# An mLSTM input projection as a first phase of seven products for eight, through DRAM

## The chip, the cores and the metric

The kernel runs on one core of one Trainium2 chip. The time of a run is the device time in microseconds (us). The metric is the median of a few runs: 2351.81 us before the change (three runs, 2350.69 to 2352.87 us). Engines are named as in the profile: PE is TensorE's matmul, PEld its weight load, DVE VectorE, ACT ScalarE, POOL GpSimd, and SP the engine whose queue issues nearly all DMAs.

## What is computed

The reference is a decoder trunk of two layers over 2048 tokens of width 1024, all in float32. Layer 0 has an mLSTM mixer, layer 1 a dilated attention over a shared K/V; after each mixer a gated embedding is added ("ple"). Cut to what the change touches:

```python
proj = rms_norm(h, norm_g) @ w_in            # 1024 -> 4104 columns
qk, v, o, z, gates = split(proj, [1024, 2048, 3072, 4096])
qk = silu(causal_depthwise_conv(qk, conv_w)) # 4 taps over tokens
q, k = split(qk, 2)                          # 4 heads of 128
ht = mlstm_chunkwise(q, k, v, i_pre, log_sigmoid(f_pre))
ht = rms_norm(sigmoid(o) * ht, hnorm_g)
h = h + (ht * silu(z)) @ w_out

def ple_add(h, p_l, ...):                    # after each mixer, p_l of width 256
    return h + (p_l @ w_proj) * sigmoid(rms_norm(h) @ w_gate)
```

## The kernel before, in words

Every large product is done in three matmuls for one: an operand is cut in a high part (`wh`, `xh`, float32r, written by ScalarE) and the rest (`wl`, `xl`, by VectorE), and TensorE adds `wh*xh`, `wl*xh` and `wh*xl` (helper `split`, lines 101 to 107; `project`, lines 150 to 173). A matmul has a 128x128 stationary operand and 512 moving columns. `project` runs over the pieces k of the inner dimension, loads and splits one 128x512 piece of the weights in each step, far ahead of its use (`high_priority(offset=PRE)`), and does 4 x 3 matmuls with it into four PSUM banks. There are eight banks. After each step it calls `pump()`, which takes one step of a generator in the list `side`: so work of another kind (mLSTM, attention) is written between two steps of a product. `drain()` takes all the steps that are left, with no product between them.

The program is written in this rough order, and the framework's scheduler sets each engine's own order from it, by priorities and by a model of its own:

- For each of four groups of 512 tokens: `a_in` (lines 323 to 432) projects the input to q, k (feature-major), the gates with a third of z, v, o and the rest of z (token-major, 344 columns a piece, `ZN`); the mLSTM of the group's four chunks of 128 tokens (`mlstm_pre`, `mlstm`) is pumped beside the products of v, o and z. `a_out` (lines 552 to 565) does the output product `w_out_a` (`mix_out`) and the embedding of layer 0 (`ple`: gate product `w_pg`, then the small product `w_p` of inner size 256). `b_in` (lines 581 to 644) projects to the shared K/V and to queries and z of layer 1, which go to DRAM.
- Beside the `b_in` of the last group and after it runs the attention; then, for each group, `mix_out` and `ple` of layer 1. In the very last `ple` the product `w_p` is written bank by bank (`by_tile`, lines 135 to 148).

In one chunk of the mLSTM, VectorE does a row part with scans (lines 470 to 483), the decay matrix (line 503, four instructions), two 512-wide products (497, 514) and, for each of four heads, the state (529), two small ones (532, 533) and the output (535); for each half the norm (546). TensorE does three 257-column matmuls for each head (525, 526, 528). A chunk's matmuls need the state of the chunk before.

Of the kernel before, what the change touches and what calls it, by code (L numbers as in the profile page):

```python
# [8 lines left out]
F32 = mybir.dt.float32  # L9
# [5 lines left out]
P = 128  # L15
# [9 lines left out]
ZN = 344  # L25
# [18 lines left out]
def trunk_kernel(ctx: ExitStack, tc: tile.TileContext, I: dict, O: dict, upto: int = 9):  # L44
# [23 lines left out]
    ready = {}  # L68
    with tc.high_priority(offset=2 * PRE):
# [22 lines left out]
    h2d = scratch("h2d", [NG, KD, P, T])  # L92
    kd = scratch("kd", [SEQ, 512])
# [40 lines left out]

    def by_tile(src, n, X, scale):

        W = []
        for k in range(len(X)):
            with tc.high_priority(offset=PRE):
                W.append(weights(src[k], n, scale))  # L140
        acc = []
        for i in range(NT):
            acc.append(bank())
            cs = slice(i * P, (i + 1) * P)
            for k, ((wh, wl), (xh, xl)) in enumerate(zip(W, X)):
# [45 lines left out]
    def sumsq(dst, src):  # L191
        jk = sm.tile([P, 512], BF16, name="jk", tag="jk", bufs=1)
        n = src.shape[-1]
        nc.scalar.activation(jk[:, :n], src, AF.Square, accum_out=dst)  # L194

    def pj(n=512):
        return sm.tile([P, n], F32, name="pj", tag="pj", bufs=8)

    def squares(acc, k, src, eng=nc.gpsimd):
# [3 lines left out]
        else:  # L203
            sq = sm.tile([P, T], F32, name="sq", tag="sq", bufs=2)
# [3 lines left out]
    def new_acc():  # L208
        return sm.tile([P, T], F32, name="acc", tag="acc", bufs=2)
# [10 lines left out]
    def spread(rst):  # L220
# [6 lines left out]
        for r in (rh.bitcast(F32), rl):  # L227
            dg = sm.tile([P, NT, P], F32R, name="dg", tag="sq", bufs=2)
# [5 lines left out]
    def row_rstd(parts, tag="rb"):  # L234
# [4 lines left out]
        rb = sm.tile([P, T], F32, name="rb", tag=tag, bufs=1)  # L239
# [31 lines left out]
    def ple(l, g, h, X, sq, done, hooks1={}):  # L271
        pT = []
        for k in range(2):
            with tc.high_priority(offset=PRE):
                praw = raw_piece(I["pT"][l, g, k], T)
                pT.append(new_x())
                split(*pT[k], praw, 1.0)
        st = {}
        hooks = rstd_hooks(st, sq, R1, R2)
        for grp in range(2):  # L280
# [9 lines left out]
            if (l, g, grp) == (1, NG - 1, 1):  # L290
                acc = by_tile(I["w_p"][l, grp], 512, pT, 0.5)
            else:
                acc = project(I["w_p"][l, grp], 512, 2, pT, True, 0.5)
            with tc.high_priority(offset=EVAC):
                for i in range(NT):
                    k = grp * NT + i
                    nc.vector.scalar_tensor_tensor(ths[i], ths[i], 1.0, acc[i], op0=ALU.add, op1=ALU.mult)
# [3 lines left out]
    pa = ExitStack()  # L301
    ap = pa.enter_context(tc.tile_pool(name="ap", bufs=1))
    tail = ap.tile([P, KD, 3], F32, name="tail")
    nc.vector.memset(tail, 0.0)
    cstate = ap.tile([P, NH, DV + 1], F32, name="cstate")
    nc.vector.memset(cstate, 0.0)
    mcar = ap.tile([NH, 1], F32, name="mcar")
    nc.vector.memset(mcar, 0.0)
    CQK = 0.25 * P ** -0.5

    ahead = {}

    def norms(g):

        sq = new_acc()
        for k in range(KD):
            raw = wp.tile([P, T], F32, name="xraw", tag="xraw", bufs=2)
            nc.sync.dma_start(raw, I["xT"][g, k])
            squares(sq, k, raw)
        ahead[g] = st = {}  # L320
        return rstd_hooks(st, sq, N1, N2, "rba")

    def a_in(g):
        X = []
        if g == 0:
            sq = new_acc()
        for k in range(KD):
            with tc.high_priority(offset=PRE):
                raw = raw_piece(I["xT"][g, k], T)
                X.append(new_x())  # L330
                split(*X[k], raw, gam[:, G_A, k:k + 1])
                if g == 0 and k < W0:
                    ready[k] = weights(I["w_q"][k], 512, 1.0)
                if g == 0:
                    squares(sq, k, raw, nc.vector)
        if g == 0:
            constants()
        if g:
            st, hooks = ahead.pop(g), {}
        else:  # L340
            st = {}
            hooks = rstd_hooks(st, sq, 5, 7)
        qk = ap.tile([P, 2 * NH, T], F32, name="qk", tag="qk", bufs=1)
        for s, seg in enumerate(("q", "k")):
            acc = project(I["w_" + seg], 512, 8, X, True, hooks=hooks if s == 0 else {})
            rst, rb = st["r"], st["rb"]
            us = []
            with tc.high_priority(offset=EVAC):
                for i in range(NH):
                    ct = s * NH + i  # L350
                    u = pj(T + 3)
                    us.append(u)
                    nc.gpsimd.tensor_copy(u[:, 0:3], tail[:, ct])
                    nc.vector.tensor_tensor(u[:, 3:], acc[i], rb, op=ALU.mult)
                    nc.gpsimd.tensor_copy(tail[:, ct], u[:, T:])
            for i in range(NH):
                ct = s * NH + i
                u = us[i]
                cv = pj()
                nc.scalar.mul(cv, u[:, 0:T], convw[:, ct, 0:1])  # L360
                for j in range(1, 4):
                    nc.vector.scalar_tensor_tensor(
                        cv, u[:, j:j + T], convw[:, ct, j:j + 1], cv, op0=ALU.mult, op1=ALU.add)
                nc.scalar.activation(u[:, 0:T], cv, AF.Tanh, scale=0.5)
                nc.vector.scalar_tensor_tensor(qk[:, ct], u[:, 0:T], 1.0, cv, op0=ALU.add, op1=ALU.mult)

        half = sm.tile([P, NT], F32, name="halfa", tag="halfa", bufs=2)
        nc.vector.tensor_scalar_mul(half, rst, 0.5)
        z = ap.tile([P, NT, DM], F32, name="z", tag="z", bufs=1)
        ga = sm.tile([P, NT, 8], F32, name="ga", tag="ga", bufs=2)  # L370

        def zproj(grp, hooks={}):
            acc = project(I["w_z"][grp], ZN, 8, X, False, hooks=hooks)
            w = ZN if grp < 2 else ZN - 8
            c0 = grp * ZN
            with tc.high_priority(offset=EVZ):
# [44 lines left out]
        for t in range(NT):  # L421
            times(t, 0, ZN)
# [503 lines left out]
```

## Time and profile before

| what | value |
| --- | --- |
| median of the runs | 2351.81 us |
| profiled execution: its own time, its span | 2347.66 us, 2345.8 us |
| granted TensorE clock, mean | 0.997 |
| busy: PE, DVE, ACT, POOL | 99%, 66%, 48%, 25% |
| DMA: bytes, mean rate | 337.14 MB, 144 GB/s |

The span runs from the first to the last instruction. "Busy" counts the union of an engine's instructions; consecutive matmuls overlap in the records, so the pace of TensorE is read from the starts of matmuls and not from their durations. In a group's row, "xcount" is the number of instructions, then come the busy time, the mean duration in ns, and the idle time of the engine ahead of them.

### The profile page before, as it was taken

How to read it: one execution, taken by the hardware profiler on the slowest of the kernel's cores; microseconds unless marked ns; L12 is line 12 of the kernel's file. 1: busy time of each engine (PE TensorE's matmuls, PEld its weight loads, DVE VectorE, ACT ScalarE, POOL GpSimd, SP SyncE). 2: the span in 40 equal slices, each digit the busy share in tenths (PEclk: the TensorE clock that was granted, in tenths of full speed). 3: DMA queues.
4: the chain of work that ended last, by engine and by line, in shares of the span. 5: the costliest groups of instructions: out<-in, count | busy, mean ns of one | idle time of the engine just before them, and what ended most of it. 6: DMA issues, size and time to landing. Idle time of an engine off the chain costs nothing.

```text
span 2345.8 us, 35374 instructions
## 1 busy us (share of the span) xinstructions
PE 2313.6 (99%) x11760; PEld 1977.5 (84%) x11760; DVE 1543.6 (66%) x3405; ACT 1128.3 (48%) x2731; POOL 593.0 (25%) x719
## 2 busy tenths in 40 slices
PE   9999999999999999999999999999999998999999
PEld 7889888888888888889888888888898887888887
DVE  6846665776566667747575675566755668786866
ACT  5434454543344545434444543344664666453643
POOL 5011235601211644011225601212202121220301
PEclk9999999999999999999999999999999999999999
DMA  5433344533244455333344543253674777465453
GB/s 184 125 91 115 99 149 162 183 116 121 61 123 125 146 164 165 117 91 111 103 130 142 174 125 120 64 171 117 203 221 134 231 237 228 135 198 164 145 160 98
DMA packets 190246, 337.14 MB, mean 144 GB/s; under 512 B 21552, under 2 KB 38256, under 8 KB 190064
## 3 DMA queue, kind: packets, MB, share of 16 engines
q1 hardware_dynamic: 189920, 334.86, 46.1%
q8 instruction: 93, 1.52, 0.3%
q14 instruction: 89, 0.73, 0.1%
q10 hardware_dynamic: 144, 0.02, 0.0%
HBM read 284.27 MB, written 50.53 MB: 143 GB/s over the span
## 4 chain that ended last, share of the span: by engine, by line
PE 85%; DVE 6%; DMA 4%; POOL 2%; ACT 2%; issue 1%; SPq 0%; ACTq 0%; DVEq 0%; POOLq 0%
PE bank L169 41%; PE bank L167 32%; PE bank L726 2%; PE bank L695 2%; PE bank L664 1%; DVE wl L104 1%; PE bank L525 1%; PE bank L526 1%; PE bank L528 1%; PE bank L715 1%; PE bank L182 1%; DMA oo<-o2d 1%; PE bank L512 1%; DMA o2d<-ot 1%; DVE xl L106 1%
## 5 line engine op out<-in xcount | busy, mean ns | idle before, releaser
L169 PE MATMUL bank<-wh,xh 128*128 128x512 f32 (+1 forms) x1664 | 642.5, 386 | 2.8 <-ACT wh L102 2.8
L169 PE MATMUL bank<-wl,xh 128*128 128x512 f32 (+1 forms) x1664 | 622.0, 374 | 0.8 <-DVE wl L104 0.8
L169 PE MATMUL bank<-wh,xl 128*128 128x512 f32 (+1 forms) x1664 | 622.6, 374 | 0.0
L102 ACT ACTIVATE wh<-wraw 128x512 fp32r<-128x512 f32 (+1 forms) x544 | 326.7, 603 | 549.5 <-PE bank L167 302.8
L104 DVE TENSOR_TENSOR wl<-wraw,wh 128x512 fp32r<-128x512 f32 (+1 forms) x512 | 353.9, 695 | 318.7 <-ACT wh L102 317.3
L167 PE MATMUL bank<-xh,wh 128*128 128x512 f32 x1272 | 501.9, 395 | 0.4 <-ACT xh L102 0.4
L167 PE MATMUL bank<-xh,wl 128*128 128x512 f32 x1272 | 496.0, 390 | 0.0
L167 PE MATMUL bank<-xl,wh 128*128 128x512 f32 x1272 | 495.9, 390 | 0.0
L169 PEld LDWEIGHTS bank<-wh,xh 128*128 128x128 f32 x1664 | 313.9, 189 | 51.0 <-ACT wh L102 3.1
L169 PEld LDWEIGHTS bank<-wh,xl 128*128 128x128 f32 x1664 | 313.4, 188 | 50.3
L169 PEld LDWEIGHTS bank<-wl,xh 128*128 128x128 f32 x1664 | 314.2, 189 | 49.3 <-DVE wl L104 1.2
L206 POOL TENSOR_TENSOR acc<-acc,sq 128x512 f32<-128x512 f32 x105 | 162.1, 1545 | 546.7 <-ACT sq L205 543.8
L167 PEld LDWEIGHTS bank<-xl,wh 128*128 128x128 f32 x1272 | 239.1, 188 | 50.5
L167 PEld LDWEIGHTS bank<-xh,wh 128*128 128x128 f32 x1272 | 239.4, 188 | 48.3 <-ACT xh L102 0.6
L167 PEld LDWEIGHTS bank<-xh,wl 128*128 128x128 f32 x1272 | 239.6, 188 | 47.8
L106 DVE SCALAR_TENSOR_TENSOR wl<-wraw,gam,wh 128x512 fp32r<-128x512 f32 x192 | 159.8, 833 | 154.1 <-ACT wh L102 151.5
L102 ACT ACTIVATE wh<-wraw,gam 128x512 fp32r<-128x512 f32 x192 | 138.0, 721 | 195.2 <-PE bank L169 134.8
L707 ACT ACTIVATE pr<-pr,nm 128x256 f32<-128x256 f32 (+1 forms) x192 | 86.6, 453 | 43.5 <-DVE nm L704 43.3
L601 POOL TENSOR_SCALAR ssb<-ssb,r 128x4 f32<-128x4 f32 x64 | 27.3, 426 | 254.1 <-ACT jk L194 233.0
L695 PE MATMUL bank<-kT,qT 128*128 128x128 f32 x600 | 78.5, 278 | 7.0 <-DVE pT L719 2.9
L695 PEld LDWEIGHTS bank<-kT,qT 128*128 128x128 f32 x600 | 72.8, 192 | 10.5 <-DVE pT L719 4.5
L726 PEld LDWEIGHTS bank<-vt,pT 128*128 128x128 f32 x600 | 75.3, 194 | 3.9
(413 smaller groups left out, 2957.4 us busy)
## 6 DMA issues: line engine op xcount, KB each, us to landing
wraw<-in_w_pg SPq DMA_DIRECT2D x128, 256.0 KB, 2.8
wraw<-in_w_in_b SPq DMA_DIRECT2D x128, 256.0 KB, 2.8
wraw<-in_w_z SPq DMA_DIRECT2D x96, 172.0 KB, 2.3
wraw<-in_w_v SPq DMA_DIRECT2D x64, 256.0 KB, 2.6
wraw<-in_w_o SPq DMA_DIRECT2D x64, 256.0 KB, 2.7
wraw<-in_w_out_a SPq DMA_DIRECT2D x64, 256.0 KB, 2.6
wraw<-in_w_kv SPq DMA_DIRECT2D x64, 256.0 KB, 2.7
kr<-kd SPq DMA_DIRECT2D x53, 256.0 KB, 4.2
```

The lines of the kernel that those rows point to most:

```text
L102: nc.scalar.mul(dst_h, src, scale)
L104: nc.vector.tensor_tensor(dst_l, src, dst_h.bitcast(F32), op=ALU.subtract)
L106: nc.vector.scalar_tensor_tensor(dst_l, src, scale, dst_h.bitcast(F32), op0=ALU.mult, op1=ALU.subtract)
L167: nc.tensor.matmul(acc[i], w[:, cs], x, start=first, stop=last)
L169: nc.tensor.matmul(acc[i][:, :n], x[:, cs], w, start=first, stop=last)
L182: nc.tensor.transpose(tp[:, t * P:(t + 1) * P], tiles[t][:, k * P:(k + 1) * P], ident)
L206: eng.tensor_tensor(acc, acc, sq, op=ALU.add)
L512: nc.tensor.matmul(sp[:, h * P:(h + 1) * P], qk[:, NH + h, ts_], qk[:, h, ts_], start=True, stop=True)
L601: nc.gpsimd.tensor_scalar(ss, ss, r2[:, t:t + 1], EPS, op0=ALU.mult, op1=ALU.add)
L695: nc.tensor.matmul(sp[:, hh * n + j * P:hh * n + (j + 1) * P], qT[:, hs], kvs[j]["k"][:, hs], start=True, stop=True)
L707: nc.scalar.activation(pr[:, hh, :n], pr[:, hh, :n], AF.Exp, bias=nm[:, h:h + 1], accum_out=md[:, 4 + h:5 + h])
L726: nc.tensor.matmul(op[:, hs], pTs[h // 2][:, c0 + j * P:c0 + (j + 1) * P], kvs[j]["v"][:, hs], start=j == 0, stop=j == nk - 1)
```

## The change

The projection (q, k, v, o, z of all tokens) moves ahead of everything else, into a phase of its own. It works on 1024 tokens at a time (`sb`) and on 1024 output columns at a time (`i`: q and k, z, o, v), inner size 1024. Each such product of 2x2 quarters (512 tokens, 512 inner, 512 columns) is made of seven quarter products instead of eight, numbered 1 to 7 and done in the order 1, 2, 5, 6, 7, 3, 4 (`PR`). The operands are sums and differences of quarters: those of x are made once for each `sb` and kept (`x_operand`), those of the weights for each product, on GpSimd (5, 7) and VectorE (6, 4) (`w_operand`), one product ahead. The results of 1, 5 and 6 are read from the running banks (`first`) and added later; finished tiles are scaled, passed through tanh where z and o need it, and written to DRAM (`ud`, `vad`, `oad`, `zad`). The gates have small products of their own (`gates`). The halves of a weight operand (128x1024 each, two for each product) have three buffers.

The small products `w_p` of both layers are moved too: those of layer 0 to the start of the first phase (`p_product`), those of layer 1 behind the first phase (`side_products`); their results go to DRAM (`pwd`), and `ple` loads them. Behind the first phase, the mLSTM of group 0 (`mixer(0)`) is pumped beside `side_products` and the rest of it is drained; `mixer(g + 1)` is pumped beside `a_out` and `b_in` of group g. A mixer loads its input from DRAM, four convolution taps included.

The core of the diff (line numbers that the text gives for new code are those of the changed file):

```diff
+    def x_operand(sb, p, accs):
+        ps = (5, 6) if p == 6 else (p,)
...
+        for kh in range(2):
+            ks = slice(2 * kh, 2 * kh + 2)
+            def put(q, t):
+                halves(new[q][0][:, ks], new[q][1][:, ks], t)
...
+            elif p == 6:
+                t, u = x_quarter(sb, 1, 0, kh, accs), x_quarter(sb, 1, 1, kh, accs)
+                nc.gpsimd.tensor_tensor(t, t, u, op=ALU.add)
+                put(5, t)
+                v = x_quarter(sb, 0, 0, kh)
+                sub(t, t, v, nc.vector)
+                put(6, t)
...
+    def w_operand(B, p):
+        out = []
+        for kh in range(2):
+            b = {(kq, nq): B[kq, nq, kh] for kq in range(2) for nq in range(2)}
...
+            elif p == 5:
+                t = b[0, 0]
+                sub(t, b[0, 1], t, nc.gpsimd)
+            elif p == 6:
+                t = B["t2", kh] = so.tile([P, 2, T], F32, name="t2", tag="t2", bufs=2)
+                sub(t, b[1, 1], b[0, 0], nc.vector)
...
+            out.append(w_half(t))
+        return out
+    def w_half(t):
+        hi, lo = (so.tile([P, 2, T], F32R, name=f"w{n}", tag=f"w{n}", bufs=3) for n in "hl")
+        halves(hi, lo, t)
+        return hi, lo
+    def multiply(X, W, acc, i, feat, first, last):
+        cs = slice(i * P, (i + 1) * P)
+        n = 2 * len(W)
+        for k in range(n):
+            wh, wl = (w[:, k % 2] for w in W[k // 2])
+            xh, xl = (x[:, k] for x in X)
+            for j, (w, x) in enumerate(((wh, xh), (wl, xh), (wh, xl))):
+                a, b = (w[:, cs], x) if feat else (x[:, cs], w)
+                nc.tensor.matmul(acc, a, b, start=first and k == 0 and j == 0,
+                                 stop=last and k == n - 1 and j == 2, skip_group_check=True)
...
+    p_weights(0)
+    for g in range(2):
+        p_operand(0, g)
+    x_operand(0, 1, accs[0])
...
+    p_product(0, 2)
+    p_product(0, 3)
+    fetch(0)
+    for p in (7, 3, 4):
+        x_operand(0, p, accs[0])
+    token_norm(0, accs[0])
+    for n, (sb, i, p) in enumerate(order):
+        with tc.high_priority(offset=60):
+            fetch(n + 1)
...
+        for j in range(NT):
+            multiply(XS[sb, p], W, dst[j], j, i == 0, start, stop)
+            with tc.high_priority(offset=EVAC):
+                if p in HALF:
+                    part[p, j] = first(HALF[p], j, dst[j])
+                else:
+                    h, nq, q = OUT[p]
+                    final(h, nq, j, dst[j], part.pop((q, j)) if q else None)
+        if i == 3 and sb == 0:
+            with tc.high_priority(offset=60):
+                x_operand(1, p, accs[1])
...
     def ple(l, g, h, X, sq, done, hooks1={}):
-            if (l, g, grp) == (1, NG - 1, 1):
-                acc = by_tile(I["w_p"][l, grp], 512, pT, 0.5)
-            else:
-                acc = project(I["w_p"][l, grp], 512, 2, pT, True, 0.5)
...
+                    pw = bg.tile([P, T], F32, name="pw", tag="pw", bufs=2)
+                    nc.sync.dma_start(pw, pwd[l, g, k])
+                    nc.vector.scalar_tensor_tensor(ths[i], ths[i], 1.0, pw, op0=ALU.add, op1=ALU.mult)
...
+    side.append(mixer(0))
+    for g in range(NG):
+        side_products(1, g)
+    drain()
+    Y, turn = turner(0)
+    turn(0, 1)
+    for g in range(NG):
+        hooks = {}
+        if g + 1 < NG:
+            side.append(mixer(g + 1))
+        X, sq = a_out(g, Y, turn)
+        if g + 1 < NG:
+            Y, turn = turner(g + 1)
+            b_in(g, X, sq, hooks=begin(Y, turn))
```

Where instructions stand now. First TensorE, in the mLSTM of group 0. Before, a head's three matmuls (lines 525, 526, 528) stood between steps of the product with the weights of o (line 169):

```order
L169 MATMUL bank<-wh,xl 128x512
L525 MATMUL bank<-v,ml 128x257 [waits Activation_49]
L526 MATMUL bank<-cstate,ml 128x257 [waits Pool_49]
L528 MATMUL bank<-v,ml 128x257 [waits Activation_49]
L169 MATMUL bank<-wh,xh 128x512
L169 MATMUL bank<-wl,xh 128x512 [waits DVE_49]
L169 MATMUL bank<-wh,xl 128x512
```

In the changed kernel this is the same place of group 0, in the drain behind the first phase (lines 697, 698 and 700 are a head's matmuls, 633, 634, 661, 667 and 684 those that prepare the next chunk):

```order
L697 MATMUL bank<-va,ml 128x257 [waits DVE_49]
L698 MATMUL bank<-cstate,ml 128x257
L700 MATMUL bank<-va,ml 128x257 [waits Activation_49]
L697 MATMUL bank<-va,ml 128x257 [waits DMAHW4_49,DVE_49,PE_49]
L698 MATMUL bank<-cstate,ml 128x257 [waits Pool_49]
L700 MATMUL bank<-va,ml 128x257
L633 MATMUL bank<-ident,gall 4x128 [waits Activation_49]
L634 MATMUL bank<-ident,gall 4x128
L697 MATMUL bank<-va,ml 128x257
L698 MATMUL bank<-cstate,ml 128x257
L700 MATMUL bank<-va,ml 128x257 [waits Activation_49]
L661 MATMUL bank<-ident,ra__5812 128x4 [waits DVE_49]
```

The products with 512 columns that stood between the heads are gone from this place: from the last 36 matmuls of `side_products` on, three of the four chunks follow each other alone. Second, SP's queue at the start. Before, the loads of x and of the first weights stood first in it:

```order
L111 DMA wraw<-in_xT 128x512
L111 DMA wraw<-in_w_q 128x512
L111 DMA wraw<-in_xT 128x512
L111 DMA wraw<-in_w_q 128x512
L111 DMA wraw<-in_xT 128x512
L78 DMA convw<-in_conv 128x32
L111 DMA wraw<-in_w_q 128x512 [waits DMAHW1_49,DVE_49,Activation_49]
```

In the changed kernel the first weights of the seven products (line 363) stand behind the loads of x (line 304) and the last stores of `p_product` (line 482):

```order
L304 DMA xr<-in_xT 128x2x512 [waits DMAHW5_49,DVE_49]
L482 DMA pwd<-st 128x512 [waits DMAHW6_49]
L482 DMA pwd<-st 128x512 [waits DMAHW7_49,Activation_49]
L482 DMA pwd<-st 128x512 [waits DMAHW0_49,DVE_49]
L482 DMA pwd<-st 128x512 [waits DMAHW1_49,Activation_49]
L482 DMA pwd<-st 128x512 [waits DMAHW2_49,DVE_49]
L482 DMA pwd<-st 128x512 [waits DMAHW3_49,Activation_49]
L482 DMA pwd<-st 128x512 [waits DMAHW4_49,DVE_49]
L482 DMA pwd<-st 128x512 [waits DMAHW5_49,Activation_49]
L363 DMA b_593<-in_s_in_a 128x1024 [waits DMAHW6_49]
L363 DMA b_595<-in_s_in_a 128x1024 [waits DMAHW7_49]
```

What the first of the seven products needs is now issued only when the load and the stores ahead of it have had their waits.

More of the change, by code (lines that the diff above doesn't have):

```diff
@@ new lines, in trunk_kernel, with sub, halves, stile @@
+    CQK = 0.25 * P ** -0.5
+    p1 = ExitStack()
+    xs = p1.enter_context(tc.tile_pool(name="xs", bufs=1, reuse_waits="tile"))
+    so = p1.enter_context(tc.tile_pool(name="so", bufs=1, reuse_waits="tile"))
+    banks = [bank() for _ in range(8)]
+    XS = {}
+    def sub(out, a, b, eng):
+        eng.tensor_tensor(out, a, b, op=ALU.subtract)
+    def halves(hi, lo, t):
+        nc.scalar.copy(hi, t)
+        nc.vector.tensor_tensor(lo, t, hi.bitcast(F32), op=ALU.subtract)
+    def stile():
+        return so.tile([P, T], F32, name="st", tag="st", bufs=10)
@@ new lines, in gate_weights, with gates @@
+    def gate_weights():
+        nc.sync.dma_start(wg, I["w_g"])
+        tmp = so.tile([P, 4, 8], F32, name="wgt", tag="wgt")
+        sub(tmp, wg[:, 4:8], wg[:, 0:4], nc.vector)
+        for q, t in enumerate((wg[:, 0:4], wg[:, 4:8], tmp)):
+            halves(wgs[:, q, :, 0:8], wgs[:, q, :, 8:16], t)
+    def gates(sb, h):
+        acc = banks[4 + h]
+        todo = ((XS[sb, 1], 0), (XS[sb, 2], 1)) if h == 0 else ((XS[sb, 5], 0), (XS[sb, 4], 2))
+        for q, (X, w) in enumerate(todo):
+            for k in range(4):
+                for j in range(2):
+                    nc.tensor.matmul(acc[0:16], wgs[:, w, k], X[j][:, k], start=q + k + j == 0,
+                                     stop=q == 1 and k == 3 and j == 1, skip_group_check=True)
+        t = stile()[0:16]
+        nc.scalar.copy(t, acc[0:16])
+        return t
@@ L434, in log_forget @@
+    p1.close()
     def log_forget(ga):
@@ L644, in b_in @@
                 nc.sync.dma_start(zd[rows(t), :], th)
-    for g in range(NG - 1):
-        b_in(g, *a_out(g, *a_in(g)))
-    X, sq = a_out(NG - 1, *a_in(NG - 1))
-    pa.close()
+    pb = ExitStack()
+    p2 = ExitStack()
+    ctx.enter_context(p2)
+    work(p2)
+    ap = pb.enter_context(tc.tile_pool(name="ap", bufs=1, reuse_waits="tile"))
+    cstate = ap.tile([P, NH, DV + 1], F32, name="cstate")
+    nc.vector.memset(cstate, 0.0)
+    mcar = ap.tile([NH, 1], F32, name="mcar")
+    nc.vector.memset(mcar, 0.0)
@@ new lines, in side_products @@
+    def side_products(l, g):
+        pT = []
+        for k in range(2):
+            with tc.high_priority(offset=PRE):
+                praw = raw_piece(I["pT"][l, g, k], T)
+                pT.append(new_x())
+                split(*pT[k], praw, 1.0)
+        for grp in range(2):
+            acc = project(I["w_p"][l, grp], 512, 2, pT, True, 0.5)
+            with tc.high_priority(offset=EVAC):
+                for i in range(NT):
+                    b = pj()
+                    (nc.scalar.copy if i % 2 else nc.vector.tensor_copy)(b, acc[i])
+                    nc.sync.dma_start(pwd[l, g, grp * NT + i], b)
```

443 lines of the change are left out of this document (277 added, 166 removed).

## The prediction

> **What bounds the kernel now.** I read the page first, then the windows by stage, then the chain of waits and the rows of single matmuls.
>
> ```profile
> span 2345.8 us, 35374 instructions
> PE 2313.6 (99%) x11760; PEld 1977.5 (84%) x11760; DVE 1543.6 (66%) x3405; ACT 1128.3 (48%) x2731; POOL 593.0 (25%) x719
> GB/s 184 125 91 115 99 149 162 183 116 121 61 123 125 146 164 165 117 91 111 103 130 142 174 125 120 64 171 117 203 221 134 231 237 228 135 198 164 145 160 98
> ```
>
> TensorE is busy for all but 32 us of the span, so a matmul less is time less, as long as nothing else comes to the front. The windows show where the 32 us are: the first `a_in`, and then a whole period of one group (from one turning of z to the next):
>
> ```profile
> core 0: us, PE busy (x) PEld busy (x) DVE busy (x) ACT busy (x) POOL busy (x), PEclk, DMA share, GB/s
> 0.00:226.50 226.50, 219.60 (x1089) 190.81 (x1090) 147.19 (x345) 99.42 (x216) 56.65 (x95) 0.98 0.41 123
> 226.50:666.80 440.30, 440.26 (x2097) 373.00 (x2097) 283.31 (x546) 203.37 (x473) 133.36 (x169) 1.00 0.42 130
> ```
>
> A period has no idle TensorE at all, with VectorE at 283/440. The pace of TensorE is in a row of the chain (start, us, line, count) and in two rows of the timeline that stand 54 matmuls apart, in the 344-column product:
>
> ```profile
> 681.74 43.57 PE bank L167 x192
> ```
>
> ```profile
> 65.72 0.32 PE L169 MATMUL bank<-wl,xh 128*128 128x344 f32 x1
> ...
> 74.00 0.32 PE L169 MATMUL bank<-wl,xh 128*128 128x344 f32 x1
> ```
>
> So a 512-column matmul costs 43.57/192 = 0.2269 us and a 344-column one 8.28/54 = 0.1533 us, whatever their durations say.
>
> **TensorE's saving.** Removed: q, k, v and o, 4 groups x 6 pieces x 8 steps x 12 = 2304 matmuls of 512, 522.8 us, and z with the gates, 1152 of 344, 176.6 us; together 699.4 us. Added: 2 x 4 x 7 products x 48 = 2688 matmuls and 64 for the gates, 2752 x 0.2269 = 624.4 us, and some 3 us of small transposes. That is **-72 us**. The 384 matmuls of `w_p` (87 us) only move, and so does the mLSTM.
>
> **Behind the first phase.** Here I see the largest price. From the last of the seven products to `w_out_a` of group 0, TensorE has 192 matmuls of `side_products` (43.6 us), four chunks of mLSTM and two turnings. The three matmuls of one head of a chunk stand here:
>
> ```profile
> 152.40 0.59 PE L525 MATMUL bank<-v,ml 128*128 128x257 f32 x2
> 152.83 0.60 PE L526 MATMUL bank<-cstate,ml 128*128 128x257 f32 x2
> 153.26 0.60 PE L528 MATMUL bank<-v,ml 128*128 128x257 f32 x2
> ```
>
> Starts are 0.43 us apart, so a head takes 1.3 us and a chunk 5.2, with some 1.7 of small ones 6.9 us; in all TensorE has 43.6 + 27.6 + 0.9 = 72 us. VectorE's work in the same stretch goes by these groups (count, busy and mean ns; I divide busy by count) and by the first and last of the eight row instructions of a chunk:
>
> ```profile
> L104 DVE TENSOR_TENSOR wl<-wraw,wh 128x512 fp32r<-128x512 f32 x416 | 304.7, 736 | 267.8 <-ACT wh L102 266.8
> L362 DVE SCALAR_TENSOR_TENSOR pj<-pj,convw 128x512 f32<-128x512 f32 x96 | 69.5, 761 | 0.1
> L365 DVE SCALAR_TENSOR_TENSOR qk<-pj 128x512 f32<-128x512 f32 x32 | 22.5, 715 | 3.8 <-ACT pj L364 3.5
> L666 DVE COPY qT<-bank 128x512 f32<-128x512 f32 x48 | 32.9, 686 | 5.8 <-PE bank L664 4.7
> L529 DVE SCALAR_TENSOR_TENSOR cstate<-cstate,dec,bank 128x257 f32<-128x257 f32 x64 | 30.1, 470 | 0.0
> L535 DVE SCALAR_TENSOR_TENSOR o<-bank,dn,o 128x256 f32<-128x256 f32 x64 | 30.8, 481 | 1.4
> L503 DVE SCALAR_TENSOR_TENSOR ml<-br,cols,masks 128x128 f32<-128x128 f32 x64 | 34.9, 602 | 27.0 <-DMA br<-rowd 27.0
> L546 DVE TENSOR_SCALAR o<-o,rr 128x256 f32<-128x256 f32 x64 | 20.0, 350 | 0.9
> L497 DVE SCALAR_TENSOR_TENSOR ml<-bank,cols 128x512 f32<-128x512 f32 x16 | 11.1, 692 | 6.5 <-PE bank L495 6.5
> ```
>
> ```profile
> 100.50 0.41 DVE L470 TENSOR_TENSOR_SCAN rb__1008<-ones,bank 4x128 f32<-4x128 f32 x1 [0.56 <-PE bank L462]
> ...
> 103.49 0.21 DVE L483 TENSOR_SCALAR rg__1011<-rg__1011 4x128 f32<-4x128 f32 x1
> ```
>
> One chunk: row part about 2.3, decay 2.2, two of 0.69, four heads at 0.47 + 0.48 + about 0.3 (5.0), norms 4 x 0.31 and small ones (2.0), and the product of z and o over 1024 columns, about 1.4 by line 104 doubled: 14.5 us, 58 for four. The convolution of group 0: 8 x (3 x 0.72 + 0.70) = 23 us; most of group 1's, which VectorE's order puts in here too: 22 taps and 6 ends, 20 us. `side_products`: 24 low parts at 0.72 (17 us), 16 results copied out of PSUM at 0.69 (11 us). Five low parts of `w_out_a` and a memset: 5 us. Sum 134 us, against TensorE's 72: this stretch is VectorE's. It begins only when the first phase's tiles are free and SP has issued the loads behind the last stores, 4 us by this row of the DMA issues (256 KB, 2.8 us) with ScalarE's first step behind it:
>
> ```profile
> wraw<-in_w_pg SPq DMA_DIRECT2D x128, 256.0 KB, 2.8
> ```
>
> With 10 us for waits of chunk on chunk the stretch takes 148 us: **+76 us** of idle TensorE. Bounds: 134 us without waits or entry (+62), 168 with waits doubled and 6 us more (+96).
>
> **Hand-overs in the first phase.** A product lasts 48 x 0.2269 = 10.9 us. Its second weight half takes the buffer that the product before it leaves six matmuls before its own end, and is needed six matmuls after the start: 12 x 0.2269 = 2.7 us for a ScalarE copy and a VectorE subtraction of 1024 columns. From 344 and 512 columns:
>
> ```profile
> L102 ACT ACTIVATE wh<-wraw 128x512 fp32r<-128x512 f32 x448 | 280.2, 628 | 474.4 <-PE bank L167 286.5 <-PE bank L169 116.2 <-issue 48.3
> L102 ACT ACTIVATE wh<-wraw 128x344 fp32r<-128x344 f32 x96 | 46.5, 486 | 75.1 <-PE bank L169 58.0 <-PE bank L167 16.4
> L206 POOL TENSOR_TENSOR acc<-acc,sq 128x512 f32<-128x512 f32 x105 | 162.1, 1545 | 546.7 <-ACT sq L205 543.8
> ```
>
> the copy is about 1.06 us, the subtraction 1.3 to 1.4 by line 104: it just fits. It no longer fits when GpSimd is at work, as VectorE's rows show, the first alone, the last beside GpSimd's:
>
> ```profile
> 269.30 0.69 DVE L104 TENSOR_TENSOR wl<-wraw,wh 128x512 fp32r<-128x512 f32 x1 [2.03 <-ACT wh L102]
> ...
> 272.42 1.73 DVE L104 TENSOR_TENSOR wl<-wraw,wh 128x512 fp32r<-128x512 f32 x1
> ```
>
> ```profile
> 272.01 4.99 POOL L206 TENSOR_TENSOR acc<-acc,sq 128x512 f32<-128x512 f32 x3 [15.42 <-ACT sq L205]
> ```
>
> The same instruction took 1.04 us longer. In the first phase GpSimd has 32 subtractions of 1024 columns (3.1 us each, line 206 doubled), some 56 scalings and additions of results and 14 squares (1.5 each) and 4 longer ones, about 220 of 610 us, 0.36. Of 56 hand-overs 20 meet it, at 0.9 us each: **+18 us**, bounds 0 and 62 (each waits out a whole subtraction). The Trainium skill, SBUF — State Buffer, section Who interferes with whom, has it as an exclusive lock: a VectorE instruction with two SBUF inputs and a GpSimd one that reads SBUF wait for each other's whole instruction; the trace agrees with blocking (1.73 for 0.69 us), and by that rule at its worst the term would be the 62 us.
>
> **The start.** `a_in` of group 0 takes 226.5 us; by count it has 576 x 0.2269 = 130.7, 288 x 0.1533 = 44.2, four chunks at 6.9 = 27.6 and some 3.5 of small ones, 206 in all, so 20.5 us go in its start-up. Now the first products need two loads of 512 KB for one of 256, and the sixth x operand has three tiles in three buffers: load 4, four squares at 1.5 us on GpSimd, its addition 3.1, two splits, some 15 us for each half behind ten earlier tiles (about 30 us). SP stands in that queue, so the first weights are issued at about 62, land at 66 and are split at 68 us; 43.6 of this are `w_p` products. 24.4 for 20.5: **+4 us**, bounds -8 and +20. Quarter 3 of the first tokens (x operands on VectorE and GpSimd), norm rows and gate columns: **+4**, 0 to 10.
>
> **`a_out` beside a mixer.** Three times the mLSTM of the next group now stands beside `a_out` and the first K/V product, 480 matmuls, with its own 27.6 us some 140 us of TensorE. What VectorE has there without it is read from the first window, what a loaded VectorE costs from the second:
>
> ```profile
> 262.00:345.00 83.00, 83.00 (x376) 69.00 (x375) 56.59 (x77) 40.29 (x69) 22.57 (x15) 1.00 0.44 134
> 1950.00:2100.00 150.00, 143.83 (x825) 124.00 (x824) 118.88 (x344) 78.99 (x197) 27.36 (x19) 1.00 0.59 184
> ```
>
> 56.59/83 over 110 us is 75 us, with 58 of mixer 133 of 140: 0.95. At 0.79 TensorE idles 4%. I take 4% here, 6 us a group: **+18 us**, bounds -3 and 45.
>
> **The end.** The last `w_p` product covered tanh and sums of the last gate product:
>
> ```profile
> 2333.53 2.73 DVE L287 TENSOR_TENSOR pj<-bank,rb 128x512 f32<-128x512 f32 x4 [4.76 <-PE bank L167]
> ...
> 2341.80 0.69 DVE L298 TENSOR_TENSOR h<-h,pj 128x512 f32<-128x512 f32 x1
> ```
>
> Before, behind the last matmul stood one bank's reading and addition (0.68 and 0.69) and the store, 3.3 us from the end of line 298 to that of the span: 4.7 us. Now the gate product's four banks end within 9 x 0.2269 = 2.0 us of each other, with twelve instructions of about 0.69 behind them: 8.3 - 2.0 + 3.3 = 9.6 us. As the first banks may be further along, I take **+4 us**, 0 to 8.
>
> At nothing: the DRAM traffic (by the tiles' sizes some 70 MB more, 30 GB/s over the span, where the slices above go from 61 to 237; uncovered it is part of the start's upper bound), and 90 more issues in SP's queue, beside 11 us of work for each product.
>
> **Sum.** -72 + 76 + 18 + 4 + 4 + 18 + 4 = +52 us. The profiled execution (span 2345.8, 1.9 us around it) would be 2399.7; it stands 4.1 under the median of the runs, so on the median 2351.8 + 52 = **2404 us**.
>
> **Rivals.** *The stretch behind the phase runs at TensorE's pace* (faster). For it: overlapping records, four of line 503 take 2.19 us for a mean of 0.602 each. Against it: 134 us are already busy time. With no idle there but the entry (+4) the time is 2332; it decides when the stretch takes under 95 us. Chance 0.20, of which 0.06 ends within 0.2% of 2351.8 (about what a measurement here can tell from no change).
>
> *TensorE's clock falls in the waits.* After a wait it was at half:
>
> ```profile
> 57.81 0.66 PE L169 MATMUL bank<-wh,xh 128*128 128x344 f32 x1 [2.83 <-ACT wh L102]
> ```
>
> ```profile
> 60.00:64.00 4.00, 4.00 (x15) 4.00 (x15) 3.30 (x6) 1.73 (x4) 0.18 (x1) 0.50 0.24 64
> ```
>
> Through the whole stretch, half speed doubles 72 us; with about 20 us of that on the chain from chunk to chunk, 2424. Chance 0.13. The Trainium skill, TensorE: Matmul & The Clock Gate, section HAM oscillation — how this bites in real kernels, says that idle gaps over about 3.4 us bring the half clock back; the trace shows it after 2.83 and 0.84 us.
>
> *Every hand-over that meets GpSimd waits out a whole subtraction:* 62 for 18 us, 2448. Chance 0.10; this is the rule of the lock above.
>
> **How the numbers follow.** The forecast has 0.57 (its own range 2375 to 2435). Slower: 0.57 + 0.13 + 0.10 = 0.80; same 0.06; faster 0.14. The range 2345 to 2455 leaves out most of the faster case and the top of the others.
>
> **What would show it.** Right: in the profile after, a stretch of about 148 us near 710 us with VectorE over 0.9 and TensorE near half; the seven products with waits for `wl` of some 1 us. Wrong: TensorE busy in that stretch; or a first phase much over 650 us; or `a_out` far longer than 146 us.

## The result and the profile after

The changed kernel takes 2537.51 us in the median of four runs (2532.66 to 2547.17), against 2352.34 us before: a ratio of 1.079 (95% interval 1.076 to 1.083), 185 us slower where the prediction had 52. The profiled execution is the longest of the four, 2547.17 us with a span of 2545.3. First the top of its page and its row of the granted clock:

```profile
span 2545.3 us, 33701 instructions
PE 2329.2 (92%) x11072; PEld 1923.4 (76%) x11072; DVE 1728.0 (68%) x3377; ACT 1166.1 (46%) x2644; POOL 745.9 (29%) x750
...
PEclk9799999999997789999899999999999999999999
```

TensorE has 688 matmuls less, and its busy time is not shorter but 16 us longer; in before it was 32 us short of the span, now it is 216. Where that is, the windows by stage show. The edges are the last of the seven products (756.1), the first `w_out_a` product (922.6), the first K/V product of groups 0 to 3 (1053.7, 1341.8, 1628.3, 1860.6) and the end, and inside the first phase the two places where x operands are made:

```profile
core 0: us, PE busy (x) PEld busy (x) DVE busy (x) ACT busy (x) POOL busy (x), PEclk, DMA share, GB/s
0.00:180.00 180.00, 147.02 (x584) 118.28 (x585) 142.01 (x141) 68.61 (x94) 83.99 (x50) 0.89 0.57 198
180.00:350.00 170.00, 170.00 (x750) 137.16 (x749) 90.38 (x123) 75.27 (x100) 52.59 (x26) 1.00 0.30 98
350.00:465.00 115.00, 98.70 (x407) 77.88 (x406) 100.76 (x98) 47.26 (x60) 42.80 (x23) 0.94 0.47 153
465.00:756.10 291.10, 291.10 (x1288) 237.18 (x1286) 137.93 (x172) 109.63 (x141) 76.43 (x41) 1.00 0.29 97
756.10:922.60 166.50, 99.06 (x367) 75.14 (x365) 116.21 (x267) 60.97 (x142) 29.00 (x66) 0.75 0.64 211
922.60:1053.70 131.10, 124.66 (x570) 100.83 (x571) 102.40 (x222) 53.75 (x124) 28.57 (x28) 0.96 0.42 137
1053.70:1341.80 288.10, 266.09 (x1177) 216.87 (x1175) 210.82 (x405) 136.03 (x350) 106.19 (x140) 0.95 0.48 156
1341.80:1628.30 286.50, 265.28 (x1175) 216.12 (x1174) 210.72 (x406) 136.45 (x351) 106.16 (x139) 0.96 0.47 154
1628.30:1860.60 232.30, 228.74 (x1024) 189.05 (x1023) 147.92 (x233) 112.11 (x279) 94.75 (x122) 0.99 0.49 157
1860.60:2545.30 684.70, 638.51 (x3745) 554.89 (x3743) 468.87 (x1318) 366.01 (x1008) 125.44 (x117) 0.98 0.59 188
```

In the steady parts of the seven products TensorE keeps its pace: 1288 matmuls in 291.1 us, 0.226 each. At the start 584 x 0.2269 = 132.5 of 180 us are matmuls, at the change of tokens 407 x 0.2269 = 92 of 115, and VectorE is busy for 0.79 and 0.88 of these. Behind the phase and beside `a_out` the clock is down too.

Three stages of the kernel before with the same edges, for the comparison (from turning z to the first K/V product; one period from K/V to K/V, which here includes an input projection; from the last K/V product to the end):

```profile
226.50:327.00 100.50, 100.46 (x459) 83.01 (x459) 65.43 (x97) 45.45 (x77) 16.50 (x12) 1.00 0.40 126
327.00:767.40 440.40, 440.35 (x2098) 373.06 (x2097) 283.40 (x547) 203.38 (x473) 133.45 (x168) 1.00 0.42 130
1646.70:2345.80 699.10, 673.94 (x3937) 585.83 (x3935) 480.77 (x1338) 377.23 (x1029) 125.05 (x117) 0.99 0.58 180
```

From these and the prediction's terms (an input projection of a group 174.8 us, `w_p` 10.9, a mixer's matmuls 27.6, all by count) the forecast of each stage can be laid beside what came:

| stage | forecast | measured | difference |
| --- | --- | --- | --- |
| first phase: 671 of matmuls + 20.5 + 26 | 717.5 | 756.1 | +39 |
| stretch behind it | 148 | 166.5 | +19 |
| `a_out` of group 0: 100.5 - 10.9 + 27.6 + 6 | 123.2 | 131.1 | +8 |
| period 0 to 1: 440.4 - 174.8 - 10.9 + 6 | 260.7 | 288.1 | +27 |
| period 1 to 2 | 260.7 | 286.5 | +26 |
| period 2 to 3, no mixer: 440.4 - 174.8 - 10.9 - 27.6 | 227.1 | 232.3 | +5 |
| rest: 699.1 - 43.6 + 4 | 659.5 | 684.7 | +25 |

The rows differ by 149 us; the profiled execution, 2547.17, lies 147.5 us above the 2399.7 forecast for it.

### The profile page after: what moved, and what is told of

Same layout as the page of the kernel before. It is cut to its first block, busy times and chain, and to the rows that moved or that the text cites. A ratio compares the mean times of both kernels' runs of the same rounds, so it can differ in the third digit from the quotient of the medians.

```text
span 2545.3 us, 33701 instructions
## 1 busy us (share of the span) xinstructions
PE 2329.2 (92%) x11072; PEld 1923.4 (76%) x11072; DVE 1728.0 (68%) x3377; ACT 1166.1 (46%) x2644; POOL 745.9 (29%) x750
## 4 chain that ended last, share of the span: by engine, by line
PE 60%; DVE 18%; DMA 8%; POOL 5%; issue 5%; ACT 3%; SPq 1%; POOLq 0%; ACTq 0%; DVEq 0%
PE bank L406 19%; PE bank L159 16%; PE bank L157 15%; PE bank L993 2%; DVE wl L109 2%; PE bank L962 2%; DMA pj<-ud 2%; DMA xr<-in_xT 1%; DVE xr L314 1%; PE bank L931 1%; DVE h L280 1%; DVE wl L111 1%; DVE xl L111 1%; DVE pj L863 1%; DMA oo<-o2d 1%
## 5 line engine op out<-in xcount | busy, mean ns | idle before, releaser
L157 PE MATMUL bank<-xl,wh 128*128 128x512 f32 x960 | 382.5, 402 | 5.0 <-DVE xl L111 3.3
L157 PE MATMUL bank<-xh,wl 128*128 128x512 f32 x960 | 384.1, 400 | 0.0
L159 PE MATMUL bank<-wh,xh 128*128 128x512 f32 x768 | 308.1, 401 | 0.0
L159 PE MATMUL bank<-wh,xl 128*128 128x512 f32 x768 | 301.9, 393 | 0.0
L159 PE MATMUL bank<-wl,xh 128*128 128x512 f32 x768 | 301.4, 392 | 0.0
L406 PE MATMUL bank<-wl,xh 128*128 128x512 f32 x672 | 264.5, 394 | 8.9 <-DVE wl L295 8.9
L406 PE MATMUL bank<-wh,xh 128*128 128x512 f32 x672 | 263.8, 393 | 7.0 <-ACT wh L294 7.0
L406 PE MATMUL bank<-wh,xl 128*128 128x512 f32 x672 | 263.7, 392 | 0.0
L107 ACT ACTIVATE wh<-wraw 128x512 fp32r<-128x512 f32 x240 | 149.8, 627 | 228.2 <-PE bank L157 171.3
L109 DVE TENSOR_TENSOR wl<-wraw,wh 128x512 fp32r<-128x512 f32 x224 | 168.4, 754 | 124.2 <-ACT wh L107 123.2
L295 DVE TENSOR_TENSOR wl<-b,wh 128x1024 fp32r<-128x1024 f32 x96 | 126.7, 1321 | 95.8 <-ACT wh L294 94.3
L159 PEld LDWEIGHTS bank<-wh,xl 128*128 128x128 f32 x768 | 145.4, 189 | 30.7
L159 PEld LDWEIGHTS bank<-wh,xh 128*128 128x128 f32 x768 | 145.8, 190 | 28.7
L406 PEld LDWEIGHTS bank<-wl,xh 128*128 128x128 f32 x672 | 127.4, 190 | 38.9 <-DVE wl L295 12.2
```

The costliest lines, as they stand in the source:

```text
L107: nc.scalar.mul(dst_h, src, scale)
L109: nc.vector.tensor_tensor(dst_l, src, dst_h.bitcast(F32), op=ALU.subtract)
L157: nc.tensor.matmul(acc[i], w[:, cs], x, start=first, stop=last)
L159: nc.tensor.matmul(acc[i][:, :n], x[:, cs], w, start=first, stop=last)
L295: nc.vector.tensor_tensor(lo, t, hi.bitcast(F32), op=ALU.subtract)
L406: nc.tensor.matmul(acc, a, b, start=first and k == 0 and j == 0, stop=last and k == n - 1 and j == 2, skip_group_check=True)
```

## The experiments

The theories: **A**, VectorE's work, spread over the whole kernel before, now stands bunched at a few places, and TensorE waits there; **B**, the chains (chunk on chunk, the way of row numbers through DRAM and back) have no cover wherever they stand; **C**, the half clock behind the waits is the larger part; **D**, the DRAM traffic behind the phase. All verdicts are medians, against the 2537.5 us of the changed kernel; stage lengths come from the profiled executions. As the changed kernel's profiled execution stands 9.7 us above its median, the gains of its stages can add up to some 10 us more than those of the medians. The stretch from the last of the seven products to the first K/V product, which several runs are compared with, is in the changed kernel:

```profile
756.10:1053.70 297.60, 223.72 (x936) 175.96 (x935) 218.61 (x488) 114.72 (x265) 57.57 (x94) 0.85 0.54 178
```

**half_pump.** The mixers at every second step of a product:

```diff
+    def halved(steps):
+        for _ in steps:
+            yield
+            yield
...
-            side.append(mixer(g + 1))
+            side.append(halved(mixer(g + 1)))
         X, sq = a_out(g, Y, turn)
```

> The mixers of groups 1 to 3 take a step only at every second step of the products, so they are spread over a_out and b_in. Theory A (VectorE's work is bunched: in the changed kernel VectorE is at 151 of 180 us beside a_out with a mixer, and at about 0.55 in the b_in behind it): of the some 37 us that TensorE loses in each of the three groups 20 to 30 go, so 2537.5 - 75 = 2460 us, 2445 to 2485. Theory B (the chain from chunk to chunk and its loads from DRAM set the pace, wherever they stand): the same waits come back between other steps, 2525 to 2545. Theory C (the half clock behind each wait is the larger part): the same as A in sign, but at most 8 us a group, 2510 to 2520.

Measured: 2493.89 us (ratio 1.061, 1.059 to 1.063), 43.6 less. The first of the two periods with a mixer in its windows, and the last period, in which no mixer begins:

```profile
1024.80:1292.90 268.10, 256.40 (x1175) 209.30 (x1174) 209.94 (x406) 132.86 (x350) 102.16 (x140) 1.00 0.52 168
...
1560.60:1809.90 249.30, 246.13 (x1123) 203.09 (x1122) 176.89 (x330) 121.41 (x319) 97.84 (x133) 1.00 0.49 160
```

The same matmuls (1175 records for 1177) with the same VectorE time (209.94 for 210.82) take 268.1 for 288.1 us: where the mixer's work stands decides, not how much of it there is. That is A in sign, but the run moves the chain too, which now has twice as many steps of a product between its own. The size is between A's and C's; the last period is 17 us longer (249.3 for 232.3), as a part of the last mixer moved into it: 1123 matmuls for 1024.

**late_mix.** The mixers only beside `b_in`:

```diff
-        if g + 1 < NG:
-            side.append(mixer(g + 1))
         X, sq = a_out(g, Y, turn)
         if g + 1 < NG:
+            side.append(mixer(g + 1))
```

> The mixers of groups 1 to 3 start only when a_out of the group before is done, so all of a mixer stands beside b_in. Theory A (VectorE's work is bunched): a_out alone loses nothing, but b_in, with VectorE at 0.55 without the mixer, now has some 100 us of mixer and convolution in about 160 us, so part of the loss only moves: 2505 us, 2480 to 2530. Theory B (chain of chunks): no gain, 2525 to 2550.

Measured: 2584.15 us (1.101, 1.098 to 1.104), 46.6 us slower than the changed kernel, which neither theory had. The longest wait of the first period stands at the beginning of the mixer. TensorE, then what VectorE waited for there:

```profile
1079.66 1.23 PE L697 MATMUL bank<-va,ml 128*128 128x257 f32 x2 [14.28 <-DVE ml L686]
```

```profile
1076.06 2.15 DVE L675 SCALAR_TENSOR_TENSOR ml<-br,cols,masks 128x128 f32<-128x128 f32 x4 [10.48 <-DMA br<-rowd]
```

TensorE stands in order behind a chunk whose row numbers are still on their way through DRAM, with VectorE idle for 10.48 us: that is B's wait. In the changed kernel the longest wait of the same period is on the same line, and it is another:

```profile
1265.13 1.23 PE L697 MATMUL bank<-va,ml 128*128 128x257 f32 x2 [8.78 <-DVE ml L686]
```

```profile
1257.91 4.16 DVE L675 SCALAR_TENSOR_TENSOR ml<-br,cols,masks 128x128 f32<-128x128 f32 x4
```

There VectorE has no pause during the whole wait: instructions for other products stand ahead of the chunk's, and the four of line 675, beside sums on GpSimd, take 4.16 us for 2.15. So beside the products both can count: A in the changed kernel, B in late_mix. What GpSimd's part is worth in this stage was not tested.

**wp1_back.** `w_p` of layer 1 in `ple` again, as in before:

```diff
-    for g in range(NG):
-        side_products(1, g)
     drain()
...
+            if l and (g, grp) == (NG - 1, 1):
+                acc = by_tile(I["w_p"][l, grp], 512, pT, 0.5)
+            elif l:
+                acc = project(I["w_p"][l, grp], 512, 2, pT, True, 0.5)
```

> The small products w_p of layer 1 stand in the last stage again, as before the change, and not behind the first phase. Theory A (VectorE sets the pace of the stretch behind the phase, and w_p covered waits of the attention at the end): the stretch is shorter by VectorE's 28 us to TensorE's 44 us; the last stage gets 43.6 us of matmuls of which some 25 fill waits: together -10 to -25, 2520 us. Theory B (the stretch is as long as the chain of chunks and its loads, the products only fill its waits): the stretch stays, the last stage is longer by 18 us, 2555 us.

Measured: 2515.29 us (1.070, 1.068 to 1.073), 22.2 less. From the last of the seven products to the first K/V product, and from the last K/V product to the end:

```profile
756.00:1001.60 245.60, 169.23 (x744) 133.62 (x743) 195.08 (x448) 92.50 (x225) 59.02 (x92) 0.83 0.47 156
...
1810.40:2518.70 708.30, 678.78 (x3937) 589.96 (x3935) 484.28 (x1342) 379.01 (x1032) 126.07 (x117) 0.99 0.56 178
```

The first is 52 us shorter (245.6 for 297.6), more than either theory gave, and the second has all of its 192 matmuls back (43.6 us) and is only 23.6 longer (708.3 for 684.7). So 20 us of `w_p` had filled waits of the attention; moving it out gave only the other half. The median is in A's range, but 52 is more than VectorE's 28 and more than TensorE's 43.6: something else was relieved. The DMA view of the first 84 us behind the phase, in the changed kernel, suggests what (issues: count, KB each, us to landing):

```profile
DMA packets 12309, 23.39 MB, mean 278 GB/s; under 512 B 1293, under 2 KB 2321, under 8 KB 12304
...
pwd<-pj SPq DMA_DIRECT2D x25, 256.0 KB, 3.7
wraw<-in_w_p SPq DMA_DIRECT2D x16, 256.0 KB, 4.8
```

This gave theory D.

**no_store.** The stores of `side_products` left out:

```diff
                     (nc.scalar.copy if i % 2 else nc.vector.tensor_copy)(b, acc[i])
-                    nc.sync.dma_start(pwd[l, g, grp * NT + i], b)
...
-                    nc.sync.dma_start(pw, pwd[l, g, k])
+                    nc.sync.dma_start(pw, pwd[0, g, k])
```

> The results of side_products are not stored (32 stores of 256 KB left out; ple of layer 1 loads those of layer 0 in their place), all else as in the changed kernel. Theory D (in the first 84 us behind the first phase 23.4 MB pass at 278 GB/s, and the loads and stores set the pace there): 8.4 MB less are 30 us less: 2508 us. Theory A (VectorE sets the pace there): its work is the same: 2530 to 2540.

Measured: 2521.67 us (1.072, 1.070 to 1.074), 15.8 less; the stretch to the first K/V product is 280.6 for 297.6 us. Half of D's 30, with VectorE's work unchanged: the stores that I had put at nothing cost some 16 us here. Whether by their traffic is not shown: they also stand in SP's queue ahead of the mixer's loads, and they keep tiles of the same eight buffers (`pj`) that these loads need. In the changed kernel's first 84 us the largest of SP's waits for a result that it is to store is this row (us in total, times, longest), and the third load of the mixer's input is issued at 788.0 us, in no_store at 776.1:

```profile
SPq L842 <- DVE pj L841: 9.9, 4, 6.8
```

**scale_act.** The scaling of x on ScalarE:

```diff
-            nc.vector.tensor_scalar(t[:, j], t[:, j], gam[:, G_A, k0 + j:k0 + j + 1], None, op0=ALU.mult)
+            nc.scalar.mul(t[:, j], t[:, j], gam[:, G_A, k0 + j:k0 + j + 1])
```

> The scaling of x by the norm's weight in the first phase (72 instructions of 128x512, mean 1.09 us beside GpSimd where the shortest take 0.40) is done by ScalarE instead of VectorE. Theory A (VectorE is what TensorE waits for at the start, 40 to 180 us, and at the change of tokens, 350 to 460 us; it loses 71 us of work there): 25 to 45 us go, 2500 us. Theory B (loads of x and GpSimd's sums set the pace there): 2530 to 2540.

Measured: 2522.73 us (1.074, 1.072 to 1.076), 14.8 less; the first phase ends at 737.7. Less than A's 25 to 45 and more than B's, and net of some 29 us of scalings that ScalarE now has in the first 180 us. The rows of the changed kernel say why these instructions were long at all. VectorE's scaling, then GpSimd in the same time:

```profile
48.56 1.61 DVE L314 TENSOR_SCALAR xr<-xr,gam 128x512 f32<-128x512 f32 x1 [0.66 <-ACT sqa L309]
50.59 4.50 DVE L314 TENSOR_SCALAR xr<-xr,gam 128x512 f32<-128x512 f32 x3 [0.42 <-ACT sqa L309]
```

```profile
48.61 1.29 POOL L310 TENSOR_TENSOR ac<-ac,sqa 128x512 f32<-128x512 f32 x1 [1.58 <-ACT sqa L309]
50.64 1.30 POOL L310 TENSOR_TENSOR ac<-ac,sqa 128x512 f32<-128x512 f32 x1 [0.74 <-ACT sqa L309]
52.30 2.52 POOL L337 TENSOR_TENSOR xr<-xr 128x1024 f32<-128x1024 f32 x1 [0.36 <-DVE xr L314]
```

The first of VectorE's takes a little longer than GpSimd's beside it and ends just behind it, and so do the last of the three and GpSimd's of line 337. So the next run takes GpSimd's work away.

**pool_free.** GpSimd's sums for operands of the first phase on VectorE, five lines in this manner:

```diff
-                sub(t, b[0, 1], t, nc.gpsimd)
+                sub(t, b[0, 1], t, nc.vector)
```

> All sums and differences that GpSimd does for operands in the first phase (and the sums of squares of x) are done by VectorE. Theory A (at the start and at the change of tokens VectorE's instructions are lengthened by GpSimd's: the scaling takes 1.09 us on the mean where the shortest take 0.40): VectorE has some 20 us more of its own work in these two places and 45 us less of lengthening: 25 us less, 2512 us, and the scalings near 0.4 us. Theory B (VectorE's amount of work alone): 2540 to 2555.

Measured: 2489.47 us (1.060, 1.058 to 1.062), 48 us less, with more work on VectorE. The same two windows and the steady part, then the scaling of the first 180 us after, in this run, and one of this run alone:

```profile
0.00:180.00 180.00, 171.13 (x734) 136.03 (x735) 148.76 (x231) 79.12 (x112) 25.20 (x20) 0.98 0.63 210
350.00:465.00 115.00, 112.34 (x496) 90.75 (x495) 84.57 (x103) 40.64 (x49) 30.41 (x14) 1.00 0.50 160
465.00:703.30 238.30, 238.30 (x1056) 193.80 (x1054) 118.55 (x159) 95.65 (x124) 25.59 (x20) 1.00 0.27 90
```

```profile
L314 DVE TENSOR_SCALAR xr<-xr,gam 128x512 f32<-128x512 f32 x42 | 48.4, 1177 | 7.5 <-ACT sqa L309 5.3 <-ACT ac L313 2.1
```

```profile
L314 DVE TENSOR_SCALAR xr<-xr,gam 128x512 f32<-128x512 f32 x42 | 23.9, 586 | 1.9 <-DMA xr<-in_xT 1.9
```

```profile
19.52 0.48 DVE L314 TENSOR_SCALAR xr<-xr,gam 128x512 f32<-128x512 f32 x1
```

In the first 180 us TensorE does 734 matmuls for 584, and VectorE 231 instructions for 141 in about the same busy time. The same 42 scalings take 586 for 1177 ns. Theory B of this run (VectorE's amount alone) would have been slower; it falls. The 48 us are not all blocking, though: GpSimd's sums were also slow links of their own (1.29 us, where VectorE's take 0.69). In the first 180 us of the changed kernel ScalarE waited for them (us in total, times, longest):

```profile
ACT sqa L309 <- POOL ac L310: 19.4, 12, 4.1
...
ACT xh L294 <- POOL xr L291: 10.0, 2, 7.0
```

The run takes both away at once and does not divide them.

**no_conv.** The three taps that VectorE computes in each convolution are left out:

```diff
-            for j in range(1, 4):
+            for j in range(1, 1):
```

> The three convolution taps that VectorE computes (24 instructions of some 0.76 us a group) are left out of all mixers; the rest stands as in the changed kernel. Theory A (VectorE's amount of work sets the pace behind the first phase and beside a_out): the stretch from the last of the seven products to the first K/V product (297.6 us), which holds 48 taps and more, loses some 35 us, and the two groups behind it some 15 each: 2470 us, 2450 to 2490. Theory B (the chain from chunk to chunk and from load to load): the taps stand ahead of the chain only for the first tiles: 2520 to 2540.

Measured: 2498.62 us (1.064, 1.062 to 1.065), 38.9 less, between the two theories. To the first K/V product 281.1 for 297.6, the two periods 274.3 and 275.1 for 288.1 and 286.5. The periods answer as A said (14 and 11 us for 18 us of taps each), the stretch does not: 16.5 us for 35. Behind the phase VectorE's amount is only about half of the story.

**warm.** Dummy matmuls in the waits behind the phase:

```diff
+    while side:
+        d = bank()
+        for _ in range(8):
+            nc.tensor.matmul(d, onesr, warm, start=True, stop=True)
+        pump()
```

> Behind the products of side_products, eight matmuls of 512 columns whose result nobody reads (1.8 us at the full clock) are written ahead of each step of mixer(0), so that TensorE has work in its waits; nothing else changes. Theory C (the half clock behind the waits costs time in this stretch, where 82 us or more pass at half clock): the clock stays up and 15 to 25 us go, 2517 us. Theory A (VectorE sets the pace there): the clock rises and the time does not fall: 2537 to 2560.

Measured: 2557.28 us (1.088, 1.086 to 1.090), 19.8 more. The same 40 us after, then in this run:

```profile
880.00:920.00 40.00, 19.41 (x71) 15.01 (x71) 34.81 (x95) 13.05 (x40) 8.25 (x11) 0.69 0.33 108
```

```profile
880.00:920.00 40.00, 40.00 (x190) 33.42 (x189) 33.21 (x91) 11.89 (x38) 5.43 (x10) 1.00 0.29 93
```

TensorE is busy at the full clock, and VectorE does its 91 to 95 instructions in the same time: in these 40 us the clock follows from the wait, and raising it gained nothing. C finds no support there; it is not excluded, as what a warm clock alone would gain, without the dummies standing ahead of the chain, is not shown.

**combo.** half_pump, wp1_back and pool_free together.

> The mixers at every second step, w_p of layer 1 back in the last stage, and GpSimd's sums of the first phase on VectorE, all three together. If the three causes are separate, as they lie at separate places, their gains add: 43.6 + 22.2 + 48.0 = 114 of the 185 us, 2423 us (2410 to 2440). If one wait only takes the place of another, less: 2445 to 2480.

Measured: 2417.96 us (1.028, 1.026 to 1.029), 119.6 less where the three alone make 113.8: the gains add, so they are separate causes. Its stretch and the end:

```profile
709.10:928.40 219.30, 146.43 (x644) 116.51 (x643) 165.62 (x353) 83.03 (x186) 52.80 (x80) 0.81 0.47 156
...
1716.70:2417.80 701.10, 675.09 (x3937) 587.21 (x3936) 483.47 (x1342) 378.89 (x1032) 126.57 (x117) 0.99 0.57 180
```

The end is back at before's 699.1. The stretch holds matmuls of 126 us (each counted at the step that most of its kind have in the trace), so 93 of its 219 are still lost.

**combo_scale.** The same with the scaling on ScalarE too.

> As the run with the three together, and the scaling of x on ScalarE too. With GpSimd out of the way 13.8 + 4.9 us are lost by TensorE's pace at the start and at the change of tokens; if VectorE's amount of work is what is left there, some 5 to 10 us go (5 to 10 below the run without it); if GpSimd's lengthening was all, none (within 3 us of it).

Measured: 2419.01 us (1.028, 1.026 to 1.030), within 1.1 us of combo. Once GpSimd is out of the way, taking the scaling off VectorE gains nothing: what scale_act gained goes back to the scaling's length beside GpSimd, not to VectorE's plain amount of work.

**combo_no_conv** is combo without the taps, by the edit of no_conv, and **combo_no_mix0** is combo without group 0's mixer (its results are left out, only z is loaded):

```diff
         mixed[g] = z
+        if g == 0:
+            for t in range(NT):
+                nc.sync.dma_start(z[:, t], zad[t * P:(t + 1) * P, :])
+            log_forget(gall[:, 0:NT])
+            return
```

> The three together, without VectorE's three convolution taps in any mixer. From the last of the seven products to the first K/V product TensorE still loses 93.2 us there. Theory A (VectorE's amount of work sets the pace of it): 35 us of taps less are 25 to 35 us less, and 5 to 10 in each of the next two groups: 2373 us, 2360 to 2385. Theory B (the chain from chunk to chunk, with the way of the row numbers through DRAM and back): 10 to 20 in all, 2398 to 2408.

Measured: 2393.12 us (1.017, 1.015 to 1.020), 24.8 less, 12 of them in the stretch (207.3 for 219.3): between the two, nearer to B. The matmuls of the first heads of each chunk in the chain of this run ("issue" is time for which the profile shows no releaser):

```profile
737.72 1.20 PE bank L730 x2
...
748.61 8.79 issue
757.40 1.20 PE bank L730 x2
...
767.05 10.45 issue
777.50 1.20 PE bank L730 x2
...
792.76 1.20 PE bank L730 x2
```

A chunk follows the one before by 15 to 20 us even without the taps, beside 14.5 us that I had counted for VectorE.

> The three together, without the convolution and the mLSTM of group 0 (only its z is loaded). If the mixer that stands alone behind the phase is what is left of the loss: TensorE's own 27.6 us and 70 to 90 us of waits go, 2310 us, below the 2353 of the kernel before even with the 27.6 added again. If the entry into the stretch (first loads, tiles that come free, first weights of w_out_a) is the larger part: 27.6 and at most 40 us, 2350 or more.

Measured: 2337.2 us (0.994, 0.992 to 0.995), 80.8 less than combo: 27.6 of matmuls and 53 of waits. The time is below the kernel before's, but with the 27.6 added it would be 2365, above it: the first of the two readings failed in size. Of its stretch, 136.5 us, 98 are matmuls, so some 38 are the entry.

## Why the prediction was wrong

The sign was right, for the reasons given in part; the size was not: +185 for +52, outside the range.

- **TensorE's saving** (-72) held: the seven products run at 0.226 us a matmul, with no wait in the steady parts.
- **The hand-overs** (+18, bounds 0 and 62) failed by place: the trace shows no wait for a weight half in 465 to 756 us. At the start and the change of tokens, which I had as +4 and +4, TensorE's waits for low halves of weights add up to 15.7 us (us in total, times, longest; 40 to 180 us, then 350 to 460):

```profile
PE bank L406 <- DVE wl L295: 6.0, 4, 2.4
...
PE bank L406 <- DVE wl L295: 9.7, 6, 2.9
```

The mechanism, GpSimd's instruction blocking VectorE's, was real, and it stood there: taking GpSimd's sums away gives 48 us (pool_free), their own slowness included. I counted quarter operands and loads there, but not the 72 scalings, whose rows the trace of before could not show, nor that GpSimd's sums would lie on many of them (median 0.90 us, shortest 0.47). The Trainium skill, SBUF — State Buffer, section Who interferes with whom, lists `tensor_scalar` among the instructions that can enter a two-port mode and then take the ports shared with GpSimd; I had used only its rule for two SBUF inputs. The runs agree on the blocking: 1.61 us beside a GpSimd sum, 0.48 alone.
- **The stretch behind the phase** (148, measured 166.5) was near in size by luck and not right in cause. VectorE is busy for 116 of it, 0.70, not over 0.9: its work is 18 us less than the 134 I had, its pauses are 50 us and not 14. In its first part the stores count (no_store, 16 us of the two stages together), as traffic or by their place in SP's queue, which I had both put at nothing; then the chain of chunks (combo_no_conv, combo_no_mix0) beside VectorE's amount. The upper bound of this term is also added up wrongly: 134, 4, 20 and 6 are 164, not 168.
- **`a_out` beside a mixer** (+18 for three groups) failed most: 8, 27 and 26 us above a forecast that had 6 each, so 79 in all for 18. I had taken 4% of TensorE's time from a stage with VectorE at 0.79, for one where it would be at 0.95. VectorE's share came out lower than that (0.78 in the `a_out` of group 0), and the loss was larger: an average share does not give these waits. half_pump gives some 20 us a period back with the same work: it stands too close, and in the changed kernel's longest wait of a period VectorE is never idle.
- **The moved `w_p`** was counted as TensorE time that only changes its place. It was also the cover of the attention at the end: 25 us above the forecast there, 20 of which wp1_back recovers.
- **The end** (+4) held: the last matmul starts at 2535.73 (the row below), 9.6 us before the end of the span, as the prediction's own sum had it.

```profile
2535.73 0.39 PE L157 MATMUL bank<-xl,wh 128*128 128x512 f32 x1
```
- **The rivals.** TensorE at its own pace behind the phase: no. The half clock: it is there (0.75 in the stretch), but in the 40 us that warm filled, raising it gained nothing. Every hand-over behind GpSimd: none in the steady parts.

What stays open: how combo's last 93 us behind the phase divide between VectorE, the loads and the chain (the taps are worth 12, the mixer 53 beside its matmuls, the entry some 38, and these overlap), how pool_free's 48 us divide between blocking and GpSimd's slow sums, and the some 9 us a period (269.2 for 260.7) that combo still stands above the forecast beside the products. Moving the first mixer into the first phase was not tried.

## What to carry to other kernels

A product that is always busy also pays for everything that stands beside it; when it is moved into a phase of its own, count each of the works that it covered at its new place, by the engine that carries it and by the length of its chain. Before an engine is given work to relieve another, look whether the two block each other: here doing GpSimd's sums on the busier VectorE saved 48 of 185 us. And how densely side work is pumped counts by itself: spread over twice as many steps, the same mixers cost 43.6 us less.

## What the runs showed of the hardware

One VectorE scaling of 128x512 with a number per partition took 0.48 us alone and 1.61 us beside a GpSimd addition of 1.29 us, ending just behind it. DMA behind the phase reached 278 GB/s over 84 us (single slices more), above the 237 of the highest slice before.
